# A hybrid attention, convolution and gating layer in split float32: first banks for the wide products, sums a tile ahead, a later first attention unit, merged sample products

## The chip, the cores and the metric

The kernel runs on one core of one Trainium2 chip. The metric is the device time of one execution in microseconds. The runs of the kernel before took 2047.26, 2047.63 and 2050.91 us; their median is 2047.63 us.

## The reference

One layer (DEPTH is 1) over a prompt of 2048 positions and over 8 sample sequences of 8 new positions each, all in float32, with a model width of 1024. The projection of the normed input is cut into three branches and their gates:

```python
q, k, v, z_a, gate_b, conv_in, z_b, u, v_c, z_c, gates = _mixer_inputs(yp, p)
y_a = _attn_prompt(q, k, v, sinks[l])          # window 128, 8 q heads, 2 kv heads, head_dim 64
conv_out, conv_last = _causal_conv(zeros, conv_in, conv_w[l])
y_c = _spatial_gate(u, v_c, w_spatial[l], b_spatial[l])
yp = _merge(yp, y_a, gate_b * conv_out, y_c, z_a, z_b, z_c, gates, p)
```

`_mixer_inputs` also norms each head of q and k (a root of the mean square over 64 values). The attention is the part that the change is about:

```python
def _sink_attend(q, k, v, dist, valid, sinks):
    s = jnp.einsum("...qkgd,...skd->...kgqs", q, k).astype(jnp.float32) * (HEAD_DIM ** -0.5)
    s = s - _alibi_slopes()[:, :, None, None] * dist.astype(jnp.float32)
    s = jnp.where(valid, s, NEG_INF)
    sink = sinks.astype(jnp.float32).reshape(N_KV_HEADS, Q_GROUP, 1, 1)
    mx = jnp.maximum(s.max(axis=-1, keepdims=True), sink)
    e = jnp.exp(s - mx)
    prob = e / (e.sum(axis=-1, keepdims=True) + jnp.exp(sink - mx))
    return jnp.einsum("...kgqs,...skd->...qkgd", prob.astype(v.dtype), v)
```

A prompt position sees the keys of its own block of 128 and of the block before it. A sample position sees its sequence's 128 cached keys and the 8 new keys of its own sequence.

## The kernel before

**Tiling.** The prompt is worked through in four blocks (SBS). Blocks 0 to 2 have four tiles of 128 positions; block 3 has four tiles and a fifth of the 64 sample positions. A block goes through kv_phase, q_phase, attention beside the za products, conv_phase, chunk_phase, gate_phase and out_phase. Large products have 512 positions as columns, in block 3 twice 288.

**Split products.** A float32 operand is cut into a high part (a cast on ScalarE, ACT, L169) and the rest (a subtraction on VectorE, DVE, L170). Each product is made of three: high times high (L178), high times low (L179) and low times high (L180). Weights arrive by DMA, are split the same way and go through a ring of four.

**PSUM.** Eight banks: three in rotation for large products (ps_mm), two for transposes and probabilities (ps_tp), and one each for the tags S0, S1 (scores) and pv (values). `wide` (L303 to L317) works on all tiles of a block at once, tile by tile for each weight unit, so it needs a bank for each tile: S0, S1, pv and then one of ps_mm (two in block 3). It serves q (`wide(2)`) and the third branch's v (`wide(6)`).

**q_phase (L399).** When a tile's last weight unit is through, head_rstd squares it on ACT (L321), sums it by head on DVE (L323) and takes the root on POOL (L165, L166); DVE then scales it to qn (L409). All of a tile's instructions are written ahead of the next tile's.

**attention (L419).** Eight units u (tile i = u // 2, key head g) in a block. A unit has four steps. queries (L438): two PE transposes (L442), then splits on ACT (L450) and DVE (L451), twice in pairs. scores (L455): eight PE products (L463, L464), bias on DVE (L466), maximum (L470, L471), exps on ACT (L474), the sink's exp (L478, L479), sum and reciprocal (L480, L481), scale (L483). probs (L485), once for each key block kb: four transposes (L488) and a split (L169, L170). values (L491): products with the high parts (L495) and with the low parts (L496).

**What sets the order.** PE and the DMA issues follow program order, which the code fixes itself by a clock: `later(delay, fn)` puts a step on a heap, and `tick(d)`, after every six products of 512 columns (0.25 a tick), emits the steps that are due. So 1.0 on this clock is 24 products. A unit's queries, scores, probs and values are due at 0.25, 1.75, 3.5 (second key block 0.5 later) and 5.25 behind 2.0 u. The za products (four output rows, L832 is their eviction on ACT) and those of conv_phase run between them. ACT, DVE and POOL are put in order by the compiler's scheduler.

**sample_attention (L519).** In block 3, during chunk_phase. For each key head g, scores(g) makes for each of the 8 sequences a product of 32 query rows with the 128 cached keys (L552) and one with the 64 new keys (L553); a bias masks what is of other sequences. values makes for each g and sequence n a product with the cached values (L593, 128 keys) and one with the new values (L594, 64 keys); the two are added up in the 64 x (4 heads x 8 positions) of that sequence. These products are plain float32, and each runs as two instructions.

Of the kernel before, what the change touches and what calls it, by code (L numbers as in the profile page):

```python
# [32 lines left out]

UNIT_EVERY = 2.0
AT_QUERIES, AT_SCORES, AT_PROBS, PROBS_EVERY, AT_VALUES = 0.25, 1.75, 3.5, 0.5, 5.25
AT_SPATIAL, SPATIAL_EVERY, SPATIAL_AFTER = 2.0, 0.3, 0.35
NEG = -1e30

# [10 lines left out]
def trunk_kernel(ctx: ExitStack, tc: tile.TileContext, A, O):  # L49
# [246 lines left out]

    def wide_outs(n, sample):

        outs = [psum.tile([P, 512], F32, tag=t, name="wide" + t, bufs=1)[:, :] for t in ("S0", "S1", "pv")]
        outs += [ps_mm()[:, :] for _ in range(n + sample - 3)]  # L300
        return [(o[:NTS] if i == n else o[:, :], NTS if i == n else P) for i, o in enumerate(outs)]

    def wide(j0, outs):  # L303
# [15 lines left out]
    def head_rstd(src, rows, nh, tag):  # L319
        sq = side("sq", [P, nh * HD])  # L320
        nc.scalar.activation(sq[:rows], src, AF.Square)  # L321
        s = small.tile([P, nh], F32, tag=tag + "s", name=tag + "s")
        nc.vector.tensor_reduce(s[:rows], sq[:rows].rearrange("p (h d) -> p h d", d=HD), AX.X, ALU.add)  # L323
        r = small.tile([P, nh], F32, tag=tag + "r", name=tag + "r")
        rstd(r[:rows], s[:rows], nh, HD)
        return r

    def kv_phase(sb, prepare):
        t0, ntile, _, sample = SBS[sb]
        if sb:  # L330
            nc.vector.tensor_copy(kst[:, :, 0, :], kst[:, :, 4, :].bitcast(F32))
            nc.vector.tensor_copy(vst[:, 0:256], vst[:, 1024:1280].bitcast(F32))
        w = nunits(0)
        abuf = res.tile([P, 4 * TMAX], F32, tag="br2h", name="abuf")
        samp = {"abuf": abuf}
        knw = abuf[:, 1024:1152]
        if sample:
            nc.sync.dma_start(knw, A["knw"])

        def keys(i, rows, kd):  # L340
            ps = ps_tp()
            for g in range(2):
                nc.tensor.transpose(
                    ps[:, g * rows:(g + 1) * rows], kd[:rows, g].rearrange("p a d -> p (a d)"), ident[:rows, :rows]
                )
            pv = ps[:, : 2 * rows].rearrange("p (g t) -> p g t", g=2)
            if i == ntile:
                kts = abuf[:, 1152:1152 + NTS]
                for g in range(2):
                    hs = slice(g * HD, (g + 1) * HD)  # L350
                    nc.scalar.activation(kts[hs], pv[hs, g], AF.Copy, scale=knw2[hs])
                samp["kts"] = kts
                return
            kk = kst[:, :, i + 1, :]
            nc.scalar.activation(kk, pv, AF.Copy, scale=knw2)
            nc.vector.scalar_tensor_tensor(kk[HD:], pv[HD:], knw2[HD:], kk[HD:].bitcast(F32), ALU.mult, ALU.subtract)

        for i in range(ntile + sample):
            rows = NTS if i == ntile else P
            if prepare and i + 1 < ntile:  # L360
                later(0.25, lambda i=i: prepare(i + 1))
            o = natural(ps_mm()[:rows, :256], i, rows, w)
            r = head_rstd(o[:, 0:128], rows, 2, "k")
            kd = tmp("kd", [P, 2, 2, HD])
            nc.vector.tensor_tensor(
                kd[:rows],
                o[:, 0:128].rearrange("p (g d) -> p g d", d=HD).unsqueeze(2).broadcast_to([rows, 2, 2, HD]),
                r[:rows].unsqueeze(2).unsqueeze(3).broadcast_to([rows, 2, 2, HD]),
                ALU.mult,
            )  # L370
            last = i == ntile
            if last or t0 + i == SEQ // P - 1:
                kvo = tmp("kvo", [P, 2, 2, HD])
                nc.vector.tensor_tensor(
                    kvo[:rows, 0], kd[:rows, :, 0, :], knw[:rows].rearrange("p (g d) -> p g d", d=HD), ALU.mult
                )
                nc.scalar.copy(kvo[:rows, 1], o[:, 128:256].rearrange("p (g d) -> p g d", d=HD))
                if last:
                    for nm, j in (("sk", 0), ("sv", 1)):
                        nc.sync.dma_start(O[nm][:, P - TS:, :], kvo[:rows, j].rearrange("p g d -> p (g d)"))  # L380
                else:
                    nc.sync.dma_start(O["pk"], kvo[:, 0].rearrange("p g d -> p (g d)"))
                    nc.sync.dma_start(O["pv"], kvo[:, 1].rearrange("p g d -> p (g d)"))
            if last:
                vs = abuf[:NTS, 1280:1408]
                nc.scalar.copy(vs, o[:, 128:256])
                samp["vs"] = vs
            else:
                b = (i + 1) * 256
                vhi = vst[:, b:b + 384].rearrange("p (g c) -> p g c", g=2)[:, :, 0:HD]  # L390
                vps = o[:, 128:256].rearrange("p (g d) -> p g d", d=HD)
                nc.scalar.copy(vhi, vps)
                nc.vector.tensor_tensor(
                    vst[:, b + 64:b + 192].rearrange("p (g c) -> p g c", g=2), vps, vhi.bitcast(F32), ALU.subtract
                )
            later(1.0, lambda i=i, rows=rows, kd=kd: keys(i, rows, kd))
        return samp

    def q_phase(sb, samp):  # L399
        _, ntile, _, sample = SBS[sb]  # L400
        qn = res.tile([P, 4 * TMAX], F32, tag="br2l", name="qn")
        abuf = samp["abuf"]
        samp["q"] = [x[:NTS, 2048:2304] for x in (qn, abuf)]
        for i, o, rows in wide(2, wide_outs(ntile, sample)):
            r = head_rstd(o, rows, 8, "q")
            for g in range(2):
                gs = slice(g * 256, (g + 1) * 256)
                dst = samp["q"][g] if i == ntile else qn[:, i * 512 + g * 256: i * 512 + (g + 1) * 256]
                nc.vector.scalar_tensor_tensor(  # L409
                    dst.rearrange("p (h d) -> p h d", d=HD),  # L410
                    o[:, gs].rearrange("p (h d) -> p h d", d=HD),
                    HD ** -0.5,
                    r[:rows, 4 * g:4 * g + 4].unsqueeze(2).broadcast_to([rows, 4, HD]),
                    ALU.mult,
                    ALU.mult,
                )
        return qn, abuf

    def attention(sb, qn, abuf, za, br, start, every):  # L419
# [87 lines left out]
        for u in range(2 * ntile):  # L507
            i, g = divmod(u, 2)
            b = slots(u)
            kbs = (0, 1) if t0 + i else (1,)  # L510
            t = start + every * u
            later(t + AT_QUERIES, lambda i=i, g=g, b=b: queries(i, g, b))
            later(t + AT_SCORES, lambda i=i, g=g, b=b, kbs=kbs: scores(i, g, b, kbs))
            for kb in kbs:
                later(t + AT_PROBS + PROBS_EVERY * kb, lambda kb=kb, b=b: probs(kb, b))
            later(t + AT_VALUES, lambda i=i, g=g, b=b, kbs=kbs: values(i, g, b, kbs))
        return sbuf

    def sample_attention(samp, sbuf, za, br):  # L519
# [24 lines left out]
        def scores(g):  # L544
# [3 lines left out]
            for n in range(NS):  # L548
                nn, j = divmod(n, 4)
                lhs = qts[gs, n * 32:(n + 1) * 32]  # L550
                rs = slice(32 * j, 32 * j + 32)
                nc.tensor.matmul(sp[rs, nn, 0:P], lhs, kc[gs, n * P:(n + 1) * P], start=True, stop=True)  # L552
                nc.tensor.matmul(sp[rs, nn, P:w], lhs, kts[gs], start=True, stop=True)  # L553
            s = sbuf[:, g * 1024:g * 1024 + 2 * w].rearrange("p (a b) -> p a b", a=2)
            nc.sync.dma_start(s, A["biass"][:, g])
            nc.vector.tensor_tensor(s, sp[:, :, 0:w], s, ALU.add)
# [26 lines left out]
        def values():  # L583
            yps = psum.tile([P, 4, NTS], F32, tag="pv", name="yps", bufs=1)
            vs = samp["vs"]
            for g in range(2):
                pts = st["p", g]
                gs = slice(g * HD, (g + 1) * HD)
                for n in range(NS):
                    nn, j = divmod(n, 4)  # L590
                    o = yps[gs, :, n * TS:(n + 1) * TS]
                    c = nn * P + 32 * j
                    nc.tensor.matmul(o, cv[:, n * P + g * HD:n * P + (g + 1) * HD], pts[:, c:c + 32], start=True, stop=False)  # L593
                    nc.tensor.matmul(o, vs[:, gs], pts[0:NTS, 256 + c:256 + c + 32], start=False, stop=True)  # L594
            ts = slice(512, 512 + NTS)
            nc.vector.tensor_tensor(zas, yps, zas, ALU.mult)
            split(br[0][0][:, :, ts], br[0][1][:, :, ts], zas)
# [363 lines left out]
```

## Time and profile before

| | us |
|---|---|
| median of three runs | 2047.63 |
| the profiled execution's own time | 2048.72 |
| its span in the trace | 2047.0 |
| DVE busy (51%) | 1050.9 |
| ACT busy (41%) | 845.8 |
| POOL busy (4%) | 83.5 |

Times in the trace count from the start of the span. A timeline row has an instruction's start and duration, engine, line, operation, output and inputs, and in brackets the idle time ahead of it with what released it. PE's instructions overlap: the step from start to start is what one costs, and it is shorter than the duration. A row with x2 holds two instructions that follow each other. A row of the windows has the stretch and its length, the busy time of PE, PEld (the weight loads), DVE, ACT and POOL with the number of instructions, the clock granted to PE (1.00 is full speed), the share of DMA and its GB/s.

### The profile page before, as it was taken

How to read it: one execution, taken by the hardware profiler on the slowest of the kernel's cores; microseconds unless marked ns; L12 is line 12 of the kernel's file. 1: busy time of each engine (PE TensorE's matmuls, PEld its weight loads, DVE VectorE, ACT ScalarE, POOL GpSimd, SP SyncE). 2: the span in 40 equal slices, each digit the busy share in tenths (PEclk: the TensorE clock that was granted, in tenths of full speed). 3: DMA queues.
4: the chain of work that ended last, by engine and by line, in shares of the span. 5: the costliest groups of instructions: out<-in, count | busy, mean ns of one | idle time of the engine just before them, and what ended most of it. 6: DMA issues, size and time to landing. Idle time of an engine off the chain costs nothing.

```text
span 2047.0 us, 27359 instructions
## 1 busy us (share of the span) xinstructions
PE 2016.7 (99%) x10887; PEld 1757.1 (86%) x10887; DVE 1050.9 (51%) x1818; ACT 845.8 (41%) x1462; POOL 83.5 (4%) x134
## 2 busy tenths in 40 slices
PE   6999999999999999999999999999999999999999
PEld 5788888888888888888888888888879999999999
DVE  5686263445588353335478535335537842533332
ACT  4675233332476333333267433333247641322320
POOL 2200000000200000000200000000110000000000
PEclk9999999999999999999999999999999998999999
DMA  6222233336222223336322223334522332222233
GB/s 206 82 83 83 84 101 123 114 119 210 84 82 83 88 78 126 111 93 201 119 83 81 84 82 109 118 108 136 173 83 59 64 114 57 65 85 86 78 104 108
DMA packets 85695, 212.25 MB, mean 104 GB/s; under 512 B 18224, under 2 KB 23344, under 8 KB 85552
## 3 DMA queue, kind: packets, MB, share of 16 engines
q1 hardware_dynamic: 85536, 209.53, 33.2%
q8 instruction: 85, 1.39, 0.3%
q10 hardware_dynamic: 32, 0.98, 0.1%
q14 instruction: 42, 0.34, 0.1%
HBM read 201.46 MB, written 10.00 MB: 103 GB/s over the span
## 4 chain that ended last, share of the span: by engine, by line
PE 93%; DVE 3%; ACT 2%; POOL 1%; issue 0%; DMA 0%; SPq 0%; ACTq 0%; DVEq 0%; POOLq 0%
PE ps_mm L179 26%; PE ps_mm L178 26%; PE ps_mm L180 26%; PE ps_tp L488 1%; PE wideS L313 1%; PE wideS L314 1%; PE wideS L312 1%; POOL qr L166 1%; PE ps_mm L312 1%; PE ps_mm L314 1%; PE ps_mm L313 1%; PE sp L464 1%; PE ps_mm L289 1%; PE ps_mm L287 1%; PE ps_mm L288 1%; PE pv L496 1%
## 5 line engine op out<-in xcount | busy, mean ns | idle before, releaser
L178 PE MATMUL ps_mm<-xh,wh 128*128 128x512 f32 (+1 forms) x2080 | 743.3, 357 | 5.0 <-DVE qn L409 4.5
L180 PE MATMUL ps_mm<-xh,wl 128*128 128x512 f32 (+1 forms) x2080 | 734.4, 353 | 0.0
L179 PE MATMUL ps_mm<-xl,wh 128*128 128x512 f32 (+1 forms) x2080 | 734.3, 353 | 0.0
L170 DVE TENSOR_TENSOR wl<-raw,wh 128x1024 fp32r<-128x1024 f32 x376 | 408.0, 1085 | 576.5 <-ACT wh L169 573.8
L169 ACT CAST wh<-raw 128x1024 fp32r<-128x1024 f32 x376 | 353.5, 941 | 772.1 <-PE ps_mm L179 535.4
L178 PEld LDWEIGHTS ps_mm<-xh,wh 128*128 128x128 f32 x2080 | 393.2, 189 | 51.9 <-issue 4.7
L180 PEld LDWEIGHTS ps_mm<-xh,wl 128*128 128x128 f32 x2080 | 392.6, 189 | 49.6
L179 PEld LDWEIGHTS ps_mm<-xl,wh 128*128 128x128 f32 x2080 | 393.4, 189 | 45.7
L179 PE MATMUL ps_mm<-ml,wh 128*128 128x512 f32 (+1 forms) x320 | 112.5, 351 | 0.3 <-DVE ml L170 0.3
L180 PE MATMUL ps_mm<-mh,wl 128*128 128x512 f32 (+1 forms) x320 | 112.4, 351 | 0.0
L178 PE MATMUL ps_mm<-mh,wh 128*128 128x512 f32 (+1 forms) x320 | 112.4, 351 | 0.0
L744 DVE TENSOR_TENSOR t<-ps_mm,t 128x512 f32<-128x512 f32 (+1 forms) x120 | 71.6, 597 | 73.7 <-PE ps_mm L180 73.7
L728 ACT ACTIVATE t<-ps_mm,c_bg 128x512 f32<-128x512 f32 (+1 forms) x120 | 73.0, 609 | 69.5 <-PE ps_mm L180 69.5
L450 ACT ACTIVATE rbuf<-ps_tp,c_qnw 64x256 fp32r<-64x256 f32 x128 | 60.0, 468 | 39.4 <-DVE rbuf L451 33.4
L179 PEld LDWEIGHTS ps_mm<-ml,wh 128*128 128x128 f32 x320 | 60.0, 188 | 8.0 <-DVE ml L170 0.6
L180 PEld LDWEIGHTS ps_mm<-mh,wl 128*128 128x128 f32 x320 | 60.1, 188 | 7.5
L178 PEld LDWEIGHTS ps_mm<-mh,wh 128*128 128x128 f32 x320 | 60.1, 188 | 7.4
L474 ACT ACTIVATE sbuf<-sbuf,nm 128x256 f32<-128x256 f32 (+1 forms) x128 | 62.8, 492 | 7.1 <-DVE nm L471 6.8
L767 DVE TENSOR_TENSOR xt<-ps_mm,xt 128x512 f32<-128x512 f32 (+1 forms) x40 | 23.9, 597 | 75.1 <-PE ps_mm L180 46.2
L179 PE MATMUL ps_mm<-br2l,wh 128*128 128x512 f32 (+1 forms) x160 | 56.5, 353 | 0.4 <-DVE br2l L170 0.2
L180 PE MATMUL ps_mm<-br2h,wl 128*128 128x512 f32 (+1 forms) x160 | 56.3, 352 | 0.0
L179 PE MATMUL ps_mm<-br1l,wh 128*128 128x512 f32 (+1 forms) x160 | 56.2, 352 | 0.0
(212 smaller groups left out, 2703.3 us busy)
## 6 DMA issues: line engine op xcount, KB each, us to landing
raw<-in_wt SPq DMA_DIRECT2D x208, 512.0 KB
raw<-in_wout SPq DMA_DIRECT2D x96, 256.0 KB
raw<-in_wn SPq DMA_DIRECT2D x40, 512.0 KB
raw<-in_wo SPq DMA_DIRECT2D x32, 512.0 KB
xbuf<-in_xn SPq DMA_DIRECT2D x12, 512.0 KB
xt<-in_xt SPq DMA_DIRECT2D x24, 256.0 KB
out_yt<-xt SPq DMA_DIRECT2D x24, 256.0 KB
xbuf<-in_xt SPq DMA_DIRECT2D x16, 256.0 KB
```

What stands on the lines that cost most here:

```text
L169: nc.scalar.copy(hi, src)
L170: nc.vector.tensor_tensor(lo, src, hi.bitcast(F32), ALU.subtract)
L178: nc.tensor.matmul(o, wh[:, ws], rh(k, c0, c1), start=k == 0, stop=False)
L179: nc.tensor.matmul(o, wh[:, ws], rl(k, c0, c1), start=False, stop=False)
L180: nc.tensor.matmul(o, wl[:, ws], rh(k, c0, c1), start=False, stop=k == kts - 1)
L312: nc.tensor.matmul(o, xh[:, k, ts], wh[:, ws], start=k == 0, stop=False)
L313: nc.tensor.matmul(o, xh[:, k, ts], wl[:, ws], start=False, stop=False)
L314: nc.tensor.matmul(o, xl[:, k, ts], wh[:, ws], start=False, stop=k == KT - 1)
L450: nc.scalar.activation(hh[half, :, e], src, AF.Copy, scale=qnw2[es])
L474: nc.scalar.activation(s[:, h, k0:], s[:, h, k0:], AF.Exp, bias=nm[:, h:h + 1], accum_out=den[:, h:h + 1])
L728: nc.scalar.activation(t[:, c0:c1], pg[:, : c1 - c0], AF.Sigmoid, bias=bg[:, 8 * b + d:8 * b + d + 1])
L744: nc.vector.tensor_tensor(t[:, c0:c1], pa[:, : c1 - c0], t[:, c0:c1], ALU.mult)
```

## The change

Four edits. (1) wide_outs hands out the ps_mm banks first and then S0, S1 and pv. (2) q_phase issues a tile's scale behind the next tile's sum. (3) The first unit of each block has its scores 0.75 later on the clock and its probabilities 0.375 later; its queries and values stay. (4) In sample_attention, the new-key scores of four sequences are one product of 128 query rows (two for each g in place of eight), and the new-value products of all eight sequences are one product of 256 columns, which starts the sum to which the eight cached-value products are added.

```diff
+FIRST_UNIT = 0.75
 def wide_outs(n, sample):
-        outs = [psum.tile([P, 512], F32, tag=t, name="wide" + t, bufs=1)[:, :] for t in ("S0", "S1", "pv")]
-        outs += [ps_mm()[:, :] for _ in range(n + sample - 3)]
+        outs = [ps_mm()[:, :] for _ in range(n + sample - 3)]
+        outs += [psum.tile([P, 512], F32, tag=t, name="wide" + t, bufs=1)[:, :] for t in ("S0", "S1", "pv")]
...
+        summed = nc.vector.tensor_reduce(s[:rows], sq[:rows].rearrange("p (h d) -> p h d", d=HD), AX.X, ALU.add)
...
-        return r
+        return r, summed
...
-        for i, o, rows in wide(2, wide_outs(ntile, sample)):
-            r = head_rstd(o, rows, 8, "q")
+
+        def scale(i, o, rows, r):
             for g in range(2):
...
+        waiting = None
+        for i, o, rows in wide(2, wide_outs(ntile, sample)):
+            r, summed = head_rstd(o, rows, 8, "q")
+            if waiting:
+                with tc.issue_after(summed.ins):
+                    scale(*waiting)
+            waiting = (i, o, rows, r)
+        scale(*waiting)
...
+            d = 0 if u else FIRST_UNIT
             later(t + AT_QUERIES, lambda i=i, g=g, b=b: queries(i, g, b))
-            later(t + AT_SCORES, lambda i=i, g=g, b=b, kbs=kbs: scores(i, g, b, kbs))
+            later(t + d + AT_SCORES, lambda i=i, g=g, b=b, kbs=kbs: scores(i, g, b, kbs))
             for kb in kbs:
-                later(t + AT_PROBS + PROBS_EVERY * kb, lambda kb=kb, b=b: probs(kb, b))
+                later(t + d / 2 + AT_PROBS + PROBS_EVERY * kb, lambda kb=kb, b=b: probs(kb, b))
             later(t + AT_VALUES, lambda i=i, g=g, b=b, kbs=kbs: values(i, g, b, kbs))
...
                 nc.tensor.matmul(sp[rs, nn, 0:P], lhs, kc[gs, n * P:(n + 1) * P], start=True, stop=True)
-                nc.tensor.matmul(sp[rs, nn, P:w], lhs, kts[gs], start=True, stop=True)
+            for nn in range(2):
+                nc.tensor.matmul(sp[:, nn, P:w], qts[gs, nn * P:(nn + 1) * P], kts[gs], start=True, stop=True)
...
+                nc.tensor.matmul(
+                    yps[gs].rearrange("p h (n t) -> p n h t", n=NS), vs[:, gs], pts[0:NTS, 256:512], start=True, stop=False
+                )
                 for n in range(NS):
                     nn, j = divmod(n, 4)
-                    o = yps[gs, :, n * TS:(n + 1) * TS]
                     c = nn * P + 32 * j
-                    nc.tensor.matmul(o, cv[:, n * P + g * HD:n * P + (g + 1) * HD], pts[:, c:c + 32], start=True, stop=False)
-                    nc.tensor.matmul(o, vs[:, gs], pts[0:NTS, 256 + c:256 + c + 32], start=False, stop=True)
+                    nc.tensor.matmul(
+                        yps[gs, :, n * TS:(n + 1) * TS],
+                        cv[:, n * P + g * HD:n * P + (g + 1) * HD],
+                        pts[:, c:c + 32],
+                        start=False,
+                        stop=n == NS - 1,
+                    )
```

The first place is DVE in block 1's q_phase. Rows give line, operation, output and inputs, and size; the number behind a tile's name tells buffers of one name apart, and the changed kernel's lines are shifted (L323 is L324 there, L409 is L410, L451 is L462, L170 is L171). Before:

```order
L323 TENSOR_REDUCE qs<-sq 128x8
L409 SCALAR_TENSOR_TENSOR qn<-wideS_4099,qr 128x256 x2
L323 TENSOR_REDUCE qs<-sq 128x8 x2
L409 SCALAR_TENSOR_TENSOR qn<-wideS_4100,qr 128x256 x2
L409 SCALAR_TENSOR_TENSOR qn<-widepv,qr 128x256 x2
L323 TENSOR_REDUCE qs<-sq 128x8
L170 TENSOR_TENSOR wl<-raw,wh 128x1024
L409 SCALAR_TENSOR_TENSOR qn<-ps_mm,qr 128x256 x2
L451 SCALAR_TENSOR_TENSOR rbuf<-ps_tp,c_qnw_153,rbuf 64x2x128 x2
```

With the change:

```order
L324 TENSOR_REDUCE qs<-sq 128x8 x2
L410 SCALAR_TENSOR_TENSOR qn<-ps_mm,qr 128x256 x2
L324 TENSOR_REDUCE qs<-sq 128x8
L410 SCALAR_TENSOR_TENSOR qn<-wideS_4100,qr 128x256 x2
L324 TENSOR_REDUCE qs<-sq 128x8
L410 SCALAR_TENSOR_TENSOR qn<-wideS_4101,qr 128x256 x2
L410 SCALAR_TENSOR_TENSOR qn<-widepv,qr 128x256 x2
L462 SCALAR_TENSOR_TENSOR rbuf<-ps_tp,c_qnw_153,rbuf 64x2x128
L171 TENSOR_TENSOR wl<-raw,wh 128x1024
```

Each sum now stands ahead of the scale of the tile before it, and the ps_mm bank is that of the first scale and no longer of the last.

The second place is ACT in block 1, between unit 0's first probabilities and the first eviction of conv_phase (cs). In both pieces the first cast to rbuf is that of the probabilities of one key block, za are the evictions of the za products, sbuf the exps of unit 1, and L450 (L461) the query splits. Before:

```order
L169 CAST rbuf<-ps_tp 128x512
L169 CAST wh<-raw 128x1024
L169 CAST rbuf<-ps_tp 128x512
L832 ACTIVATE za<-ps_mm 128x512
L450 ACTIVATE rbuf<-ps_tp,c_qnw_153 64x2x128
L474 ACT_TABLE_LOAD
L474 ACTIVATE sbuf,den<-sbuf,nm 128x256 x4
L479 ACTIVATE es<-es 128x4
L450 ACTIVATE rbuf<-ps_tp,c_qnw_153 64x2x128
L614 COPY cs<-ps_mm 128x512
```

With the change:

```order
L170 CAST rbuf<-ps_tp 128x512
L854 ACTIVATE za<-ps_mm 128x512
L461 ACTIVATE rbuf<-ps_tp,c_qnw_153 64x2x128 x2
L485 ACT_TABLE_LOAD
L485 ACTIVATE sbuf,den<-sbuf,nm 128x256 x4
L490 ACTIVATE es<-es 128x4
L461 ACTIVATE rbuf<-ps_tp,c_qnw_153 64x2x128 x2
L170 CAST rbuf<-ps_tp 128x512
L636 COPY cs<-ps_mm 128x512
```

The cast of unit 0's second probabilities stood ahead of unit 1's table load and exps, and now stands behind them and behind four query splits.

The third place is PE at the sample's values in block 3: the end of a large product, and the products with the cached values (L593, now L610) and with the new ones (L594, now L604). Before, the first two of 32 such rows that go on in turn:

```order
L178 MATMUL ps_mm<-xh,wh 128x288
L179 MATMUL ps_mm<-xl,wh 128x288
L180 MATMUL ps_mm<-xh,wl 128x288
L593 MATMUL yps<-sbuf 64x4x8
L594 MATMUL yps<-sbuf,abuf 64x4x8
```

With the change, all of them:

```order
L181 MATMUL ps_mm<-xh,wl 128x288
L604 MATMUL yps<-sbuf,abuf 64x8x4x8
L610 MATMUL yps<-sbuf 64x4x8 x8
L604 MATMUL yps<-sbuf,abuf 64x8x4x8
L610 MATMUL yps<-sbuf 64x4x8 x8
L179 MATMUL ps_mm<-xh,wh 128x288
```

Two kinds of product that took turns are now one of the one kind and eight of the other for each key head.

More of the change, by code (lines that the diff above doesn't have):

```diff
@@ L322, in head_rstd @@
         s = small.tile([P, nh], F32, tag=tag + "s", name=tag + "s")
-        nc.vector.tensor_reduce(s[:rows], sq[:rows].rearrange("p (h d) -> p h d", d=HD), AX.X, ALU.add)
+        summed = nc.vector.tensor_reduce(s[:rows], sq[:rows].rearrange("p (h d) -> p h d", d=HD), AX.X, ALU.add)
         r = small.tile([P, nh], F32, tag=tag + "r", name=tag + "r")
         rstd(r[:rows], s[:rows], nh, HD)
-        return r
+        return r, summed
     def kv_phase(sb, prepare):
@@ L362, in kv_phase @@
             o = natural(ps_mm()[:rows, :256], i, rows, w)
-            r = head_rstd(o[:, 0:128], rows, 2, "k")
+            r, _ = head_rstd(o[:, 0:128], rows, 2, "k")
             kd = tmp("kd", [P, 2, 2, HD])
```

## The prediction

> **What bounds the kernel now.** I read the page first: the span, the busy shares, and the chain that ended last.
>
> ```profile
> span 2047.0 us, 27359 instructions
> PE 2016.7 (99%) x10887; PEld 1757.1 (86%) x10887; DVE 1050.9 (51%) x1818; ACT 845.8 (41%) x1462; POOL 83.5 (4%) x134
> ...
> PE 93%; DVE 3%; ACT 2%; POOL 1%; issue 0%; DMA 0%; SPq 0%; ACTq 0%; DVEq 0%; POOLq 0%
> ```
>
> TensorE (PE) is the bound. A change can gain only where PE stops, runs at a lowered clock, or issues fewer instructions. So the next view is PE's waits by releaser; columns: total us, times, longest.
>
> ```profile
> PE ps_mm L178 <- DVE qn L409: 4.5, 1, 4.5
> PE sp L464 <- DVE rbuf L451: 2.9, 5, 1.1
> PE ps_mm L178 <- ACT za L832: 0.5, 1, 0.5
> ```
>
> The first two belong to one chain: q's products end, tile by tile ACT squares, DVE sums (L323), POOL takes the root (L165, L166), DVE scales (L409), PE transposes, ACT and DVE split (L450, L451), and PE makes the scores (L463, L464). Left out are L463's wait on L450, of the same chain, and waits on lines that the diff leaves alone. Idle time misses slow starts and lost clock, so I price each place by the starts of PE's instructions (first column start, second duration):
>
> ```profile
> 67.02 0.22 PE L463 MATMUL sp<-kst,rbuf 128*128 128x128 f32 x1
> 70.38 0.45 PE L178 MATMUL ps_mm<-xh,wh 128*128 128x512 f32 x1
> 81.59 0.22 PE L463 MATMUL sp<-kst,rbuf 128*128 128x128 f32 x1
> 82.92 0.44 PE L178 MATMUL ps_mm<-xh,wh 128*128 128x512 f32 x1
> 544.86 0.39 PE L178 MATMUL ps_mm<-xh,wh 128*128 128x512 f32 x1
> 545.54 0.28 PE L463 MATMUL sp<-kst,rbuf 128*128 128x256 f32 x1
> 548.12 0.28 PE L463 MATMUL sp<-kst,rbuf 128*128 128x256 f32 x1
> 548.59 0.40 PE L178 MATMUL ps_mm<-xh,wh 128*128 128x512 f32 x1
> 1025.12 0.28 PE L463 MATMUL sp<-kst,rbuf 128*128 128x256 f32 x1
> 1028.45 0.63 PE L178 MATMUL ps_mm<-xh,wh 128*128 128x512 f32 x1
> 1031.59 0.39 PE L180 MATMUL ps_mm<-xh,wl 128*128 128x512 f32 x1
> ```
>
> Eight score products undisturbed take twice the last four of block 1, 0.94 (548.12 to 548.59). Block 0's first scores took 3.36 and its second 1.33, so they lose 2.42 and 0.39: **2.8**. Block 1 took 3.05 and loses **2.1**. Block 2 took 3.33 and loses 2.4; then eight product steps to 1031.59 take 3.14, where a step of 0.227 (three from 544.86 to 545.54) gives 1.82: 1.3 more, **3.7** in all. The windows show why (length, busy by engine, granted clock):
>
> ```profile
> 1027.84:1031.25 3.41, 3.41 (x12) 2.83 (x11) 3.17 (x6) 2.45 (x4) 0.00 (x0) 0.50 0.26 48
> 1512.53:1519.35 6.82, 6.05 (x25) 6.08 (x26) 3.39 (x7) 2.79 (x5) 1.75 (x2) 0.50 0.20 75
> 1700.27:1710.51 10.24, 10.24 (x54) 9.13 (x53) 0.85 (x2) 0.40 (x1) 0.00 (x0) 0.50 0.00 0
> ```
>
> The clock is halved for one, two and three times 3.41 us, each time behind a stretch of PE waits or of tiny products. One lost window costs half of it, 1.7. Now block 3 and the sample's values:
>
> ```profile
> 1508.22 0.29 PE L178 MATMUL ps_mm<-xh,wh 128*128 128x288 f32 x1
> ...
> 1508.49 0.29 PE L180 MATMUL ps_mm<-xh,wl 128*128 128x288 f32 x1
> 1513.30 0.58 PE L178 MATMUL ps_mm<-xh,wh 128*128 128x288 f32 x1 [4.53 <-DVE qn L409]
> 1696.84 0.24 PE L593 MATMUL yps<-sbuf 128*64 128x32 f32 x1
> 1696.91 0.22 PE L593 MATMUL yps<-sbuf 128*64 128x32 f32 x1
> 1697.07 0.24 PE L594 MATMUL yps<-sbuf,abuf 64*64 64x32 f32 x1
> 1697.30 0.30 PE L593 MATMUL yps<-sbuf 128*64 128x32 f32 x2
> 1706.23 0.61 PE L178 MATMUL ps_mm<-xh,wh 128*128 128x288 f32 x1
> 1710.63 0.30 PE L178 MATMUL ps_mm<-xh,wh 128*128 128x288 f32 x1
> ```
>
> A 288-column product steps 0.135 (1508.22 to 1508.49). In block 3 a za product waits 4.53 for a bank that q's last tile still holds; start to start that is 4.81 − 0.135 = 4.7. Then the window of 6.82 at clock 0.50 holds 25 products in 6.05, 0.24 each: 25 × 0.105 = 2.6. The wait on za's eviction (L832) follows from ACT starting late on the same chain: 0.5. Together **7.8**.
>
> **The change part by part.** *Banks and sums ahead.* They act on one chain, so I price them together.
>
> ```profile
> 533.55 0.20 POOL L165 TENSOR_SCALAR qr<-qs 128x8 f32<-128x8 f32 x1 [16.41 <-DVE qs L323]
> 533.83 1.64 POOL L166 TENSOR_TENSOR qr<-qr,mhalf 128x8 f32<-128x8 f32 x1
> 535.50 0.76 DVE L409 SCALAR_TENSOR_TENSOR qn<-wideS,qr 128x256 f32<-128x256 f32 x2 [2.04 <-POOL qr L166]
> 541.57 0.68 DVE L323 TENSOR_REDUCE qs<-sq 128x8 f32<-128x512 f32 x1
> 545.19 0.76 DVE L409 SCALAR_TENSOR_TENSOR qn<-ps_mm,qr 128x256 f32<-128x256 f32 x2 [1.81 <-POOL qr L166]
> ```
>
> Before, the sum of the last tile (541.57) stands behind the scale of the tile ahead of it, which waits for POOL; POOL idles, and the last scale ends at 545.95. With sums ahead POOL works without gaps: a small step and a root take 1.92 (533.55 to 533.83, and 1.64), so from 533.55 the four end at 535.5, 537.4, 539.3 and 541.2; the last scale (0.76) ends near 542.1, about 3.9 earlier. The scores' last stop ended just ahead of 548.12; 3.9 earlier is 544.2, ahead of their old place. The large products' banks were those of the last tiles and are now those of tile 0 (in block 3 of tiles 0 and 1): block 3's 4.5 goes, since the first scale stands 9.7 ahead of the last (535.50, 545.19). Removed: 2.8 + 2.1 + 3.7 + 7.8 = **16.4**. What the swap adds costs nothing: the bank that block 3's second tile takes over has kv's split of the values (L393) as its last reader, and tile 0's six products, 6 × 0.227 = 1.4, stand between; without that cover PE would stop until that read ends.
>
> *FIRST_UNIT.* Scores go 18 products later (4.1), to about 549.8 in block 1: 5.6 behind their operands. So 0.75 is more than is needed, and it has a price: probabilities move too, but values don't. Unit 0's second cast now stands on ACT behind unit 1's table load, its four exps and two pairs of unit 2's query splits.
>
> ```profile
> 552.72 1.28 ACT L474 ACT_TABLE_LOAD   x1
> ...
> 556.21 0.95 ACT L450 ACTIVATE rbuf<-ps_tp,c_qnw 64x256 fp32r<-64x256 f32 x2
> 545.86 0.47 DVE L451 SCALAR_TENSOR_TENSOR rbuf<-ps_tp,c_qnw,rbuf 64x256 fp32r<-64x256 f32 x1
> 556.63 0.88 DVE L483 TENSOR_SCALAR sbuf<-sbuf,den 128x256 f32<-128x256 f32 x3
> 564.70 0.68 DVE L170 TENSOR_TENSOR rbuf<-ps_tp,rbuf 128x512 fp32r<-128x512 f32 x1
> 570.79 0.39 PE L496 MATMUL pv<-rbuf,vst 128*128 128x512 f32 x1
> ```
>
> Before, the low half was there at 565.4 and its product came at 570.8: 5.4 of slack. After, from unit 2's transposes: 0.5 until the first pair of splits starts, 0.95 for it, 3.49 for table load and exps (552.72 to 556.21): 4.9. From there DVE needs 0.2 + 0.4 for the sums, 1.2 for four scalings, 0.47 for the last split and 0.68 for the low half: 7.9 if one follows the other, 7.5 with the overlap that the rows show (556.63 is only 0.4 behind 556.21); ACT's cast is ready by then. PE needs the low half 24 products, five to eight transposes and three value products later: about 6.8. New wait: **0.65** in blocks 1 and 2; 0.1 in block 0, whose tile 0 has no first half; 1.65 in block 3, where a weight cast of 1.05 stands ahead of the table load and the gemm products before it are 0.135. Sum **3.1**. Bounds: nothing, if ACT's order gives a microsecond back; 8.2, if three of them also lose a window (3 × 1.7).
>
> *Sample scores.* 14 short products fewer of 32 a group, the wide row ones larger; at 0.08 to 0.23 a step that is worth under 0.3. I take nothing.
>
> *Sample values.* Each product runs as two instructions. 64 take 9.39 (1696.84, the first, to 1706.23). A change between the two shapes steps 0.155 and a repeat 0.075, so a sample's four take 0.46 (1696.84 to 1697.30); at the halved clock from 1700.27 more. After: 32 of one shape at 0.08 = 2.6, four new 256-column ones, and four shape changes at 0.07 extra, 0.3. The trace has no such 256-column instruction. Lower bound 0.08 each, as the 32-column one; upper bound eight of those, 0.64, if it costs by the same runs of eight outputs. The nearest 256-column row is the score at 0.117 (548.12 to 548.59 in four), and I take 0.12: 0.5. Sum 3.4, so **6.0** goes; with 0.64, and repeats at 0.115 (half of 0.23), only 2.8. The halved clock behind it: 18 products to 1710.63 took 4.40 against 18 × 0.135 = 2.4: **2.0** goes, if 3.4 us of small work don't fill a window.
>
> The page "PSUM — Partial Sum Buffer" of the Trainium skill (Specifications) says that any non-contiguous access slows matmuls significantly. It speaks against the merged product, whose output lies in runs of eight; no run here shows its price, and with 0.64 each the sum would be 2.1 worse, 2028.4.
>
> **Sum.** 16.4 + 6.0 + 2.0 − 3.1 = 21.3 against the profiled execution: span 2047.0 to 2025.7, and with the 1.7 around it (its time is 2048.7) 2027.4. The runs' median is 2047.63, 1.1 below that execution, so I give **2026.3**.
>
> **Rivals.**
> - *No new wait* at the first values: 2047.6 − 24.4 = 2023.2. For it: 5.4 of slack before. Against: ACT's new order, row by row.
> - *The sample's group keeps its clock loss or its length.* One window lost: 2028.0. None of the 8.0 gained: 2034.3. For it: the clock fell behind tiny products at 1700.27, though PE looked busy. Against: half of them go. The Trainium skill's page "TensorE: Matmul & The Clock Gate" (Part 1) has a free-running window of 3413 ns whose idle state halves the clock; the three window rows agree (3.41, 6.82, 10.24). By it a group of 3.4 loses a window only where it nearly fills one.
> - *First values lose the clock as well*: three windows, 5.1 more, 2031.4.
> - *The bank change doesn't do what it says*: block 3's product waits for another bank's reader and keeps its 7.8: 2034.1.
> - *Slower*: unit 0's postponed probabilities stop PE at the first values in all blocks. It decides from 24.4 / 4 = 6.1 a block, wait and clock together; with waits of 5.4 (as much as the former slack) and 2.6 of clock, as block 3 shows, 32.0 − 24.4 = 7.6 over: 2055. Against it: the chain above misses by 0.65, not 5.
>
> **How the numbers follow.** Forecast with its sizes off by up to a window either way: 0.56; no new wait 0.15; sample group 0.14; clock at the first values 0.08; bank change fails 0.04; slower 0.03, of which I put a third within the bound. A measurement of this kernel can tell about 0.2%, 4.1 us, from no change. Faster 0.96, same 0.02, slower 0.02. The range leaves out the far ends of the sample group and of the bank rival: 2021 to 2033.
>
> **What would show it.** Right: no PE wait on L409's or L451's outputs; clock 1.00 at the first scores of blocks 2 and 3; POOL's roots back to back; the sample's values in 3 to 4 us; and a new wait of 0.5 to 0.8 at the first L496 products of blocks 1 and 2, the longest in block 3. Wrong: a wait for qn in block 3, waits at values over 2 us, or the clock at 0.50 behind either.

## The result and the profile after

The changed kernel takes 2030.14 us (median of four runs, 2029.88 to 2031.01); the kernel before, with one more run beside it, 2048.70 us. The ratio is 0.991, with a 95% interval from 0.9898 to 0.9922: 18.6 us or 0.9% faster. The forecast was 2026.3 us, within 2021 to 2033.

The page of the changed kernel, the same lines as of before:

```profile
span 2028.4 us, 27259 instructions
...
PE 2004.4 (99%) x10835; PEld 1745.1 (86%) x10835; DVE 1051.7 (52%) x1818; ACT 846.3 (42%) x1462; POOL 79.8 (4%) x134
...
PE 94%; ACT 2%; DVE 2%; POOL 1%; issue 0%; DMA 0%; SPq 0%; ACTq 0%; DVEq 0%; POOLq 0%
```

PE's waits by releaser (total, times, longest; lines of the changed kernel, where L506 and L507 are the value products, L170 and L171 the split, L854 za's eviction):

```profile
PE pv L507 <- DVE rbuf L171: 2.4, 4, 0.7
...
PE pv L506 <- ACT rbuf L170: 0.8, 1, 0.8
PE ps_mm L179 <- ACT za L854: 0.4, 1, 0.4
```

The waits on qn and at the scores are gone. In their place stand waits of the value products for unit 0's probabilities, in every block (twice in block 3), as forecast. They are small in this view and larger by the starts of PE. I cut the trace at the same large products in every kernel and compared the lengths of the pieces, so that a slow start and a halved clock count too. In us against the profiled execution of before; the last row is the prediction:

| | up to block 0's za | block 0's units | block 1's | block 2's | block 3's | sample scores | sample values |
|---|---|---|---|---|---|---|---|
| changed kernel | −1.4 | −2.5 | −1.1 | −2.2 | −3.9 | +0.6 | −8.1 |
| changed kernel, again | +0.1 | −2.6 | −1.1 | −2.5 | −5.5 | +0.6 | −8.1 |
| predicted | 0 | −2.7 | −1.45 | −3.05 | −6.15 | 0 | −8.0 |

The first column is the start-up, which the change doesn't touch; in the traces of this study it lies between 1.4 us shorter and 2.2 us longer than in that of before. The loss against the forecast lies in the blocks' units and in the sample's scores. PE at block 1's first values and at block 3's shows the new wait (here and below, rows between those shown are left out):

```profile
564.45 0.48 PE L506 MATMUL pv<-rbuf,vst 128*128 128x512 f32 x1
565.66 0.50 PE L507 MATMUL pv<-rbuf,vst 128*128 128x512 f32 x1 [0.73 <-DVE rbuf L171]
565.99 0.39 PE L179 MATMUL ps_mm<-xh,wh 128*128 128x512 f32 x1
...
1532.47 0.40 PE L507 MATMUL pv<-rbuf,vst 128*128 128x512 f32 x1
1533.69 0.49 PE L506 MATMUL pv<-rbuf,vst 128*128 128x512 f32 x1 [0.82 <-ACT rbuf L170]
1534.92 0.50 PE L507 MATMUL pv<-rbuf,vst 128*128 128x512 f32 x1 [0.74 <-DVE rbuf L171]
```

A step of 0.23 became 1.21 in block 1 (0.73 of it idle, the rest a slow start), and the step behind it 0.33: 1.1 lost. In block 3 two such steps lose 2.0, and then the clock drops. The windows of the two profiled executions of the same code, behind that wait:

```profile
1534.90:1538.30 3.40, 3.38 (x18) 3.32 (x18) 1.02 (x3) 2.03 (x5) 0.00 (x0) 0.66 0.00 0
```

```profile
1535.50:1539.00 3.50, 2.90 (x22) 2.86 (x22) 1.60 (x4) 2.76 (x5) 0.00 (x0) 1.00 0.00 0
```

The first has a mean clock of 0.66, the second kept 1.00; that makes the 1.5 us between the two rows of the table in block 3's column.

### The profile page after: what moved, and what is told of

Same layout as the page of the kernel before. It is cut to its first block, busy times and chain, and to the rows that moved or that the text cites. A ratio compares the mean times of both kernels' runs of the same rounds, so it can differ in the third digit from the quotient of the medians.

```text
span 2028.4 us, 27259 instructions
## 1 busy us (share of the span) xinstructions
PE 2004.4 (99%) x10835; PEld 1745.1 (86%) x10835; DVE 1051.7 (52%) x1818; ACT 846.3 (42%) x1462; POOL 79.8 (4%) x134
## 4 chain that ended last, share of the span: by engine, by line
PE 94%; ACT 2%; DVE 2%; POOL 1%; issue 0%; DMA 0%; SPq 0%; ACTq 0%; DVEq 0%; POOLq 0%
PE ps_mm L180 26%; PE ps_mm L179 26%; PE ps_mm L181 26%; PE wideS L315 1%; PE wideS L313 1%; PE wideS L314 1%; PE ps_tp L499 1%; PE ps_mm L314 1%; PE ps_mm L315 1%; PE ps_mm L313 1%; PE sp L475 1%; PE sp L474 1%; PE pv L507 1%; PE widepv L313 1%; PE widepv L314 1%; PE widepv L315 1%
## 5 line engine op out<-in xcount | busy, mean ns | idle before, releaser
L171 DVE TENSOR_TENSOR wl<-raw,wh 128x1024 fp32r<-128x1024 f32 x376 | 408.3, 1086 | 574.4 <-ACT wh L170 570.7
L170 ACT CAST wh<-raw 128x1024 fp32r<-128x1024 f32 x376 | 353.6, 941 | 772.0 <-PE ps_mm L180 548.0
L461 ACT ACTIVATE rbuf<-ps_tp,c_qnw 64x256 fp32r<-64x256 f32 x128 | 59.9, 468 | 33.4 <-DVE rbuf L462 24.9
```

The lines of the kernel that those rows point to most:

```text
L170: nc.scalar.copy(hi, src)
L171: nc.vector.tensor_tensor(lo, src, hi.bitcast(F32), ALU.subtract)
L461: nc.scalar.activation(hh[half, :, e], src, AF.Copy, scale=qnw2[es])
```

## The experiments

My theory (P): the sums ahead alone bring unit 0's operands in time; FIRST_UNIT is not needed and costs the new waits; the sample's values gain what they were forecast to gain. Its rivals: the later scores are what removed the waits (Q), or the waits at the values have another cause (R).

**FIRST_UNIT at 0.**

```diff
-FIRST_UNIT = 0.75
+FIRST_UNIT = 0.0
```

> The changed kernel with FIRST_UNIT at 0: unit 0's scores and probabilities are back at their old places, the rest stays. Theory P (the sums ahead alone bring unit 0's operands in time, and the waits at the first values, 0.6 + 1.1 + 1.1 + 3.7 us in blocks 0 to 3 with the clock loss in block 3, come from the later probabilities alone): all of them go and no wait comes back at the scores, 2030.1 - 6.5 = 2023.6 us. Theory Q (the later scores are what removed the waits at the scores): those come back with 2 to 2.5 us in each of blocks 0 to 2 and the waits at the values go, so 2029 to 2032 us. Theory R (the late probabilities are late for another reason, a slower ACT behind unit 1): the waits at the values stay, 2030 us.

Measured: 2026.28 us (2025.80 to 2026.76), ratio 0.9891 (0.9876 to 0.9906). No wait is left at scores or at values: block 0's units −2.8, block 1's −2.1, block 2's −3.7, block 3's −6.9. DVE in block 1, then PE in block 1 and at block 3's two waits:

```profile
540.86 0.49 DVE L462 SCALAR_TENSOR_TENSOR rbuf<-ps_tp,c_qnw,rbuf 64x256 fp32r<-64x256 f32 x1
```

```profile
542.60 0.28 PE L474 MATMUL sp<-kst,rbuf 128*128 128x256 f32 x1
565.76 0.39 PE L507 MATMUL pv<-rbuf,vst 128*128 128x512 f32 x1
1506.82 0.40 PE L179 MATMUL ps_mm<-xh,wh 128*128 128x288 f32 x1 [0.35 <-ACT za L854]
1518.30 0.40 PE L179 MATMUL ps_mm<-xh,wh 128*128 128x288 f32 x1 [0.49 <-ACT za L854]
```

The last operand is there at 541.35 (540.86 and 0.49) and the scores start at 542.60, at their old place: 1.25 in hand, where they had waited. P holds, Q and R fall. P had the time 2.7 too low: I had taken 6.5 for the waits, where the pieces of the first profile come to 5.6 (0.2, 1.0, 1.5 and 2.9, its units less these), and 1.5 of that is the clock in block 3, which doesn't fall in every run. Two short waits on za's eviction stay in block 3.

**The sums ahead alone.** The edit is q_phase and head_rstd of the change, on the kernel before.

> The kernel before with the sums of q a tile ahead and nothing else. Theory P: the waits at the first scores of blocks 0 to 2 and block 2's clock loss go (2.8 + 2.1 + 3.7 = 8.6 us), and in block 3, where five tiles follow each other and the last scale comes only about 0.8 us earlier, the za product's wait stays near 3.7 us with its clock loss: 2048.7 - 9.4 = 2039.3 us. Theory Q (later scores did that): under 3 us gained, 2046 us or more.

Measured: 2034.19 us, ratio 0.9931 (0.9916 to 0.9945), 14.9 below the 2049.04 of the kernel before in that session. Blocks 0 to 2 give −3.0, −2.1 and −3.7 as expected, and block 3 −5.5 where I had expected −0.8:

```profile
1499.92 0.29 PE L180 MATMUL ps_mm<-xh,wl 128*128 128x288 f32 x1
1501.94 0.37 PE L178 MATMUL ps_mm<-xh,wh 128*128 128x288 f32 x1 [1.73 <-DVE qn L409]
```

The wait for the bank is 1.73 in place of 4.53, and no clock is lost behind it. I had the step mis-sized: the scale that frees the bank comes 2.8 earlier and not 0.8, because POOL stood still twice for 1.47 between block 3's roots before (ahead of 1505.05 and 1510.45) and now for 0.08. This one edit carries most of the gain outside the sample group.

**The bank order alone.** The edit is wide_outs of the change, on the kernel before.

> The kernel before with the new bank order and nothing else. Theory P: only block 3 gains, its 4.5 us wait for a bank and the 2.6 us of halved clock behind it; its first scores may wait in its place for about 1 us (the operands come as late as before): 2048.7 - 6.5 = 2042.2 us, and blocks 0 to 2 keep their waits at the scores. Rival: the wait moves whole to block 3's first scores, 2048 us.

Measured: 2047.19 us, ratio 0.9996 (0.9987 to 1.0006): no gain clear of noise, where a gain of up to 2.7 us lies within the interval. PE and ACT in block 3:

```profile
1519.95 0.40 PE L178 MATMUL ps_mm<-xh,wh 128*128 128x288 f32 x1 [3.12 <-ACT za L832]
```

```profile
1517.22 0.95 ACT L450 ACTIVATE rbuf<-ps_tp,c_qnw 64x256 fp32r<-64x256 f32 x2 [7.33 <-DVE rbuf L451]
1518.19 1.28 ACT L832 ACT_TABLE_LOAD   x1
1519.49 0.41 ACT L832 ACTIVATE za<-ps_mm 128x288 f32<-128x288 f32 x1
```

The first banks are free early now, but the next one waits for za's eviction, and that stands on ACT behind the query splits, which wait 7.33 for the same late scale. The wait has changed its name from L409 to L832; 3.12 of 4.53 are left, so 1.4 went. Block 3's units are 2.6 shorter in this trace: those 1.4, and for most of the rest one window of lost clock in place of two. The windows vary by themselves: the kernel with the sample's edits alone, with the old bank order, also lost only one there, and both lost one in the start-up and one in block 0, where the kernel before lost none. My place for the moved wait (the scores) was wrong.

**The sample's edits alone.** The edit is sample_attention of the change, on the kernel before.

> The kernel before with the sample's merged scores and merged new values and nothing else. Theory P: the values take 3.2 us in place of 9.4 and the halved clock behind them (2.0 us) goes, the scores take 1.15 us a group in place of 0.83: 2048.7 - 6.2 - 2.0 + 0.65 = 2041.2 us. Rival (the clock loss hangs on where the group lies in a window): a window is lost, 2042.9 us.

Measured: 2041.81 us, ratio 0.9963 (0.995 to 0.9975), 0.6 above the expected 2041.2. Scores +0.6, values −8.1, as in the changed kernel. None of the seven traces with merged values lost clock behind them; the four without lost two or three windows each.

**The changed kernel again.**

> The changed kernel once more, beside the next three on the same chip: 2030 us if it agrees with its first runs; its start-up (up to block 0's za products), 1.3 us shorter than in most other traces, should be the usual length again if that was chance, and then 2031 us.

Measured: 2030.44 us (2029.72 to 2031.03), with the usual start-up and no lost clock in block 3: in the first profile the short start-up and the lost clock had cancelled out by chance.

**Unit 0's values moved too.**

```diff
-            later(t + AT_VALUES, lambda i=i, g=g, b=b, kbs=kbs: values(i, g, b, kbs))
+            later(t + AT_VALUES + (0 if u else 0.2), lambda i=i, g=g, b=b, kbs=kbs: values(i, g, b, kbs))
```

> The changed kernel with unit 0's values also moved, by 0.2 on the clock: 6 products later in blocks 0 to 2 (1.4 us), 12 of 288 columns (1.6 us) in block 3. Theory P (the waits at the first values come from probabilities that moved while the values did not): the waits of blocks 0 to 2 (0.3 to 1.1 us) go whole, block 3 keeps about 0.5 us of 2.1 and no clock loss, 5 us less than the changed kernel on the same chip. Theory R (the moved step makes ACT late by itself): the wait follows the values, under 1.5 us gained.

Measured: 2026.81 us (2025.51 to 2028.34), 3.6 below the changed kernel on the same chip; ratio to before 0.9896 (0.9881 to 0.991). Blocks 0 to 2 lose nothing at the values any more, and block 3 keeps one wait:

```profile
566.96 0.39 PE L507 MATMUL pv<-rbuf,vst 128*128 128x512 f32 x1
```

```profile
1533.38 0.50 PE L507 MATMUL pv<-rbuf,vst 128*128 128x512 f32 x1 [0.73 <-DVE rbuf L171]
```

So the waits are the distance between moved probabilities and unmoved values (P). The gain fell short of 5 by about what the changed kernel had not lost this time, the clock in block 3.

**The old scores with FIRST_UNIT at 0.**

```diff
                 nc.tensor.matmul(sp[rs, nn, 0:P], lhs, kc[gs, n * P:(n + 1) * P], start=True, stop=True)
-            for nn in range(2):
-                nc.tensor.matmul(sp[:, nn, P:w], qts[gs, nn * P:(nn + 1) * P], kts[gs], start=True, stop=True)
+                nc.tensor.matmul(sp[rs, nn, P:w], lhs, kts[gs], start=True, stop=True)
```

> FIRST_UNIT at 0 and the sample's scores as before (16 products a group), the merged new values kept. Theory P (the merged scores cost 0.33 us a group, by the trace): 0.65 us less than with FIRST_UNIT at 0 alone, 2025.6 us; the two groups 0.83 us each, from large product to large product.

Measured: 2024.68 us (2024.65 to 2025.03), ratio 0.9885 (0.9868 to 0.9901); the groups are back to their old length. This is the fastest kernel of the study, 5.8 us below the changed one beside it. PE at the first group's scores, before and with the change:

```profile
1668.46 0.44 PE L552 MATMUL sps<-sbuf 64*32 64x128 f32 x8
1668.70 0.31 PE L553 MATMUL sps<-abuf,sbuf 64*32 64x64 f32 x8
1668.81 0.43 PE L552 MATMUL sps<-sbuf 64*32 64x128 f32 x8
1669.03 0.33 PE L553 MATMUL sps<-abuf,sbuf 64*32 64x64 f32 x8
1669.29 0.40 PE L178 MATMUL ps_mm<-xh,wh 128*128 128x288 f32 x1
```

```profile
1657.27 0.64 PE L565 MATMUL sps<-sbuf 64*32 64x128 f32 x16
1657.84 0.66 PE L567 MATMUL sps<-abuf,sbuf 64*128 64x64 f32 x4
1658.42 0.40 PE L179 MATMUL ps_mm<-xh,wh 128*128 128x288 f32 x1
```

Before, the sixteen instructions of the short product took 0.11 (1668.70 to 1668.81) and 0.26 (1669.03 to 1669.29, with the step to the large product); the four merged ones take 0.58, with the same step. The products with the cached keys, sixteen as before, take 0.57 in place of 0.46, with the change of shape behind them. Fewer instructions, more time.

**A new-value product with unbroken output.** On the kernel of the run before:

```diff
-            yps = psum.tile([P, 4, NTS], F32, tag="pv", name="yps", bufs=1)
+            yps = psum.tile([P, 4 * NTS], F32, tag="pv", name="yps", bufs=1)
...
-                    yps[gs].rearrange("p h (n t) -> p n h t", n=NS), vs[:, gs], pts[0:NTS, 256:512], start=True, stop=False
+                    yps[gs], vs[:, gs], pts[0:NTS, 256:512], start=True, stop=False
...
-                        yps[gs, :, n * TS:(n + 1) * TS],
+                        yps[gs, n * 32:(n + 1) * 32],
...
-            nc.vector.tensor_tensor(zas, yps, zas, ALU.mult)
+            zv = zas.rearrange("p h (n t) -> p h n t", n=NS)
+            nc.vector.tensor_tensor(zv, yps.rearrange("p (n h t) -> p h n t", n=NS, h=4), zv, ALU.mult)
```

> The kernel of the run before it with the values' sums laid out by sequence, so that each product writes an unbroken row of PSUM (256 and 32 columns) and DVE reorders when it multiplies. Theory S (writing in runs of eight is what makes the merged product dear): its step falls from 0.267 us to the 0.117 of a score product of 256 columns, the four save 0.6 us. Theory T (a plain float32 product of 256 columns costs that much however it is written): the step stays within 0.02 us of 0.267 and the time the same.

Measured: 2025.45 us (2025.01 to 2027.12), no gain. PE at the values, in runs of eight (the run before it) and unbroken; L603 and L609 are the changed kernel's L604 and L610:

```profile
1681.19 0.64 PE L603 MATMUL yps<-sbuf,abuf 64*64 64x256 f32 x2
1681.77 1.12 PE L609 MATMUL yps<-sbuf 128*64 128x32 f32 x16
```

```profile
1681.18 0.64 PE L603 MATMUL yps<-sbuf,abuf 64*64 64x256 f32 x2
1681.75 1.12 PE L609 MATMUL yps<-sbuf 128*64 128x32 f32 x16
```

Two instructions take 0.58 and 0.57 from start to start. The layout costs nothing here (T).

**FIRST_UNIT alone.** The edit is attention's loop of the change with FIRST_UNIT at 0.75, on the kernel before.

> The kernel before with FIRST_UNIT at 0.75 and nothing else. Theory P (later scores alone also cover the operands, at the price at the values): the waits at the first scores of blocks 0 to 2 go and waits of 0.3, 1.1 and 1.1 us come at the first values; block 3 keeps its 4.5 us wait for q's bank with the halved clock and gets 1.4 to 3 us more at its first values: 2048.9 - 2.6 - 1.1 - 2.4 + 2 = 2045 us. Theory Q (without the sums ahead the operands are too late even so): waits at the scores stay above 1 us in blocks 1 and 2, 2049 us or more.

Measured: 2049.72 us, ratio 1.0001 (0.9991 to 1.001): no gain. The scores wait no more, so P is right about what it covers, but its time was 4.7 too low, as I had the price too low; block 0's first values:

```profile
90.83 0.80 PE L496 MATMUL pv<-rbuf,vst 128*128 128x512 f32 x1 [2.29 <-ACT rbuf L170]
```

Block 0's wait there is 2.29, where the changed kernel has 0.2, and the clock halves behind it; blocks 1 and 2 gain 0.4 and 1.6, block 3 loses 2.7.

## Why the prediction was right, and where it was off

**The size.** The measured time lies 3.8 us above the forecast. The second profile's span of 2028.0 is 2.3 above the forecast 2025.7, and that lies in the pieces: block 3's waits (0.9 less removed), the new waits (0.7 more) and the sample's scores (0.6 more) make up nearly all. Another 1.1 is what I took off because the profiled execution of before (2048.72) stood above the median of three runs; the medians of 15 and 13 later runs, 2049.04 and 2048.38, show that it was an ordinary one, so that step rested on noise. The rest is the spread of the runs.

**Right: what goes.** In the changed kernel POOL's roots in block 1 follow each other every 2.0 us, where the prediction had 1.92, and behind the first none waits for a sum:

```profile
529.87 1.64 POOL L167 TENSOR_TENSOR qr<-qr,mhalf 128x8 f32<-128x8 f32 x1
531.86 1.64 POOL L167 TENSOR_TENSOR qr<-qr,mhalf 128x8 f32<-128x8 f32 x1
```

With FIRST_UNIT at 0 the last operand's 541.35 is 544.3 in the times of before (all is 2.94 earlier there when block 1 starts); the prediction had 544.2. The terms 2.8, 2.1 and 3.7 of blocks 0 to 2 are −2.8, −2.1 and −3.7 with FIRST_UNIT at 0, and the sums ahead alone give them. Block 3's 7.8 came to 6.9. The part of it that failed is the 0.5 for za's eviction, which I counted as gone: two such waits of 0.35 and 0.49 are left, one of them new. That the terms fit to a tenth owes something to luck: lost clock is part of them, and it is compared with the one execution from which it was read. The trace of the new bank order alone lost no window in block 2, and that block is 1.6 shorter there.

**Unexamined: which edit does it.** The prediction priced the bank order and the sums ahead as one and gave block 3's 4.5 to the banks. The runs put it the other way round: sums alone −5.5 in block 3 (2.8 of the wait, and the clock behind it); banks alone 1.4 of the wait and no gain in time clear of noise, because the next bank waits behind the same late scale through ACT; with the sums in place the banks add 1.3 (block 3's units at −5.5 without them and −6.9 with them). The rival that the bank change leaves the wait to another reader of a bank is, for 3.1 of the 4.5, what happens when it stands alone.

**Mis-sized: the new waits at the first values.** Mechanism, place and blocks were as forecast; the sum of 3.1 is 3.8 in the changed kernel's second profile (0.2, 1.0, 1.2 and 1.4, its pieces less those with FIRST_UNIT at 0) and 5.6 in the first, where block 3's wait also cost a clock window. The prediction had named a halved clock behind the values as a sign of being wrong; it came there, once in four blocks and in one of two traces, and cost 1.5 of the 5.1 that the rival on the clock at the first values had. ACT and DVE in block 1, from unit 2's transposes at 557.84:

```profile
559.30 1.28 ACT L485 ACT_TABLE_LOAD   x1
...
562.80 0.97 ACT L461 ACTIVATE rbuf<-ps_tp,c_qnw 64x256 fp32r<-64x256 f32 x2
```

```profile
563.22 1.14 DVE L494 TENSOR_SCALAR sbuf<-sbuf,den 128x256 f32<-128x256 f32 x4
564.39 0.49 DVE L462 SCALAR_TENSOR_TENSOR rbuf<-ps_tp,c_qnw,rbuf 64x256 fp32r<-64x256 f32 x1
564.91 0.69 DVE L171 TENSOR_TENSOR rbuf<-ps_tp,rbuf 128x512 fp32r<-128x512 f32 x1
```

The low half ends at 565.60, 7.8 behind the transposes, where I had 7.5. PE would have needed it at 564.68 (564.45 and a step of 0.23), 6.8 behind, as forecast. The wait's idle time is then 0.73 against 0.65; what I left out is the slow start on top, some 0.35 a wait.

**Wrong: the sample's scores.** I took nothing, within 0.3, counting short products by the steps of lone ones. In the trace the short products on different groups of 32 output rows overlap: eight of them start within 0.11, and one merged product of the same 64 columns steps 0.11 by itself (1658.00, 1658.11, 1658.22). So merging four of them saved nothing, and the steps at the changes of shape around them (0.16 to 0.20) came on top: +0.6 for the two groups.

**Right in sum, wrong in parts: the sample's values.** 6.0 + 2.0 was forecast, 8.1 measured. The 256-column instruction costs 0.285 with its change of shape (0.57 for two, from 1686.29 to 1686.86 below), where I had 0.12 and 0.07, and a repeat 0.066 in place of 0.08; that the two errors offset each other (3.24 measured against 3.4) was luck:

```profile
1686.29 0.64 PE L604 MATMUL yps<-sbuf,abuf 64*64 64x256 f32 x2
1686.86 1.12 PE L610 MATMUL yps<-sbuf 128*64 128x32 f32 x16
1687.91 0.64 PE L604 MATMUL yps<-sbuf,abuf 64*64 64x256 f32 x2
1688.48 1.12 PE L610 MATMUL yps<-sbuf 128*64 128x32 f32 x16
1689.53 0.40 PE L179 MATMUL ps_mm<-xh,wh 128*128 128x288 f32 x1
```

The rule of the Trainium skill's page "PSUM — Partial Sum Buffer" (Specifications), that a non-contiguous access slows matmuls significantly, would have made the unbroken output faster. It did not (0.58 and 0.57); for runs of eight the measurement decides against it.

What stays open: why the start-up is shorter than before's by 1.4 us in the changed kernel's first trace and by 1.1 in that of FIRST_UNIT alone; why FIRST_UNIT alone makes block 0 wait 2.29 at the values, and by what rule a wait loses clock.

## What to carry to other kernels

When a wait is removed by two edits at once, undo each: here one edit that shortens the chain did the work, and a second that makes room for the old, longer chain mostly moved the wait to the next step. A step that is postponed can fall behind other work on another engine, as unit 0's probabilities did on ACT; move the last consumer as well or leave the step where it is. Counting instructions says little of small matrix products: see in the trace which of them ran side by side before merging them.

## What the runs showed of the hardware

The same wait loses clock in one trace and none in another. In block 0 the kernel before and the one with the new bank order alone have the same wait at the first scores. The windows behind it, in this order:

```profile
72.00:77.00 5.00, 5.00 (x24) 4.10 (x24) 3.34 (x11) 4.95 (x13) 0.00 (x0) 1.00 0.43 147
```

```profile
72.00:77.00 5.00, 5.00 (x18) 4.03 (x19) 4.29 (x9) 4.85 (x6) 0.00 (x0) 0.66 0.34 105
```

In block 2 it is the other way round: the kernel before lost a window there (its row of clock 0.50 from 1027.84), the other kept 1.00:

```profile
1032.00:1035.00 3.00, 3.00 (x16) 2.48 (x15) 2.94 (x6) 2.99 (x5) 0.00 (x0) 1.00 0.47 122
```

This agrees with the free-running window of the Trainium skill's page "TensorE: Matmul & The Clock Gate" (Part 1). It may also be why the kernel before spreads over 7.7 us in 15 runs (2045.42 to 2053.16), and the three kernels with FIRST_UNIT at 0, which have no waits at scores or values, over 1.0, 0.4 and 2.1 in four runs each; the numbers of runs differ, and that was not tried by itself.
